# Six gate rows move from the attention's fill into the in-projection, and the fill becomes a fixed plan

## The chip, the cores and the metric

The kernel runs on one core of a Trainium2 chip. The metric is the device time of one execution in microseconds. A profile of one execution, taken by the hardware profiler, stands beside the times; its engines are TensorE (PE, with weight loads as PEld), VectorE (DVE), ScalarE (ACT), GpSimd (POOL) and SyncE (SP, which here issues nearly all DMAs).

## The reference

One layer of a hybrid encoder is computed for 1024 prompt frames and 32 sample frames (1056 columns, `T`), 1024 features wide, all in f32:

```
h = rmsnorm(x) * g_mix;  q,k,v,cb,cc,cx,ga,gc = split(h @ w_in)
y_attn = stick_breaking(q,k,v) @ w_attn_out            # 8 heads x 64
y_conv = (cb * causal_conv3(cc * cx)) @ w_conv_out
x = x + (sigmoid(ga) * y_attn + sigmoid(gc) * y_conv) @ w_o
x = x + square(relu(rmsnorm(x) @ w_up)) @ w_down
x = x + sigmoid(rmsnorm(x) @ w_ple_gate) * (p @ w_ple)
y = rmsnorm(x)
stick_breaking: A[t,s] = sigmoid(z[t,s]) * prod_{s<j<t} (1 - sigmoid(z[t,j])), strictly causal
```

The branch gates `ga` and `gc` are 1024 wide each: 16 rows of 128 features, numbered 0 to 15 here. Rows 0 to 7 belong to the attention branch and rows 8 to 15 to the convolution branch.

## The kernel before

Every f32 product is made of three matmuls on operands split into a high and a low part (fp32r), so one product of a 128x128 weight block with 264 columns is three `MATMUL 128x264`. Columns are taken in quarters of 264 (`TQ`).

**In-projection.** `SETS` lists pairs of 128-feature rows of `w_in`. The first two pairs (gate rows 0 to 3) are made plainly by `first_gates`. The other twelve (conv, query, key and value rows) go through `seven`, a Strassen-like scheme: seven block products of 24 matmuls each instead of eight, 168 matmuls for two rows. The scheme's weight sums are made by `prepare` on GpSimd, ScalarE and VectorE while the set before runs. `follow` queues the work on finished rows as generators in the list `side`, which `run` advances by a step after each product.

**The attention.** 64 turns, one for each pair of head and 128-query block (`steps`); turn n does, in the order `ORDER = "LSAFBFG"`: the reverse product scan of turn n-1 on VectorE (`weigh`, L782), the scores of turn n on TensorE (`scores`, L764 and L765, into one PSUM buffer `z`) with their sigmoid on ScalarE (L768) and mask on GpSimd (L775), the transposes of turn n-2 in two halves (`flip`, L818, copied by ScalarE at L821 and split by VectorE at L822), and every second turn the product with the values (`gather`, L839, evicted by ScalarE at L848 and VectorE at L1190). At the two places `F` the function `fill` puts in other TensorE work, so much as `shares()` allots to the turn. The query tiles of a turn (`queries`) are fetched by three DMAs on SP four turns ahead; the first two tiles are fetched just ahead of turn 0.

**The fill.** It is counted in units; one unit is 24 matmuls of 264 columns, a quarter of a gate row in plain form (`gate_group`, 96 matmuls a row). There are 60 units (`PIECES`): gate rows 4 to 15 (48), the eight rows of the per-layer embedding `p @ w_ple` (8), and two rows of the convolution's output projection (4, `conv_unit`, L937 to L939). `feed` and `weave` walk these units one after another: a unit's weights are loaded a unit or two ahead and split when the unit before begins. A group's PSUM buffer is one of two (`gps`), freed by a ScalarE copy (`sg` L652, `em` L726), and raw weights lie in four buffers (`wraw`, `RB = 4`). `START = 6` units run between the in-projection and the first turn. A finished gate row is stored raw to `gd`, fetched later as `sc` or `sa`, multiplied by the rows' inverse norm `rs` and put through the sigmoid (`branch_scale`, `branch_sigmoid`, or in `conv_unit` at L927 and L929).

The order on TensorE, VectorE, ScalarE and GpSimd is that of the program text. SP issues its DMAs in one queue, in order, and each issue can wait for a semaphore; eight semaphores are used in turn, so a DMA also waits until the eighth before it has landed.

Of the kernel before, what the change touches and what calls it, by code (L numbers as in the profile page):

```python
# [9 lines left out]
F32 = mybir.dt.float32  # L10
# [5 lines left out]
P = 128  # L16
# [21 lines left out]
SHB = 4  # L38
AT1 = (5, 4, 6, 7, 8, 12)
AT_IN = (4, 8, 10, 12, 14, 18)  # L40
PLAIN_GATES = 4
PIECES = 60.0
# [7 lines left out]
def tile_step(  # L50
# [506 lines left out]
    def conv_gate(nb, m):  # L557
# [10 lines left out]
        nc.sync.dma_start(cvd[nb, 1], m)  # L568
        yield

    def follow(nm, n, ms, wait=0):
        gens = []
        for p, m in zip((n, n + 1), ms):
            if nm in "qk":
                gens.append(keys_or_queries(nm, p, m))
            elif nm == "v":
                gens.append(values(p, m))
            elif nm == "cc":
                cst["cc", p] = m
                gens.append(call(scaled, m))  # L580
            else:
                gens.append({"cx": conv_in, "cb": conv_gate}[nm](p, m))
        side.extend([after(wait, gens[0]), after(wait + {"v": 6, "cx": 6, "cb": 4}.get(nm, 1), gens[1])])

    def first_gates():

# [72 lines left out]
    def gate_parts(n, raw):  # L659
        return even_odd(load_w(None, 0, KD, f"g{n}", raw=raw))  # L660

    def gate_unit(n, ahead):
        def body(w):
            sg = blk(f"sg{n}")
            for t in range(4):
                yield from gate_group(n, w, sg, t)
            nc.sync.dma_start(gd[n], sg)

        return partial(gate_fetch_, n), partial(gate_parts, n), body, (0, ahead), 4

    def last_gates(n):

        raw = []

        def prepare(r):
            raw.append(r[1])
            return gate_parts(n, r[0])

        def body(w):
            ww, sg = [w, None], [blk(f"sg{n}"), blk(f"sg{n + 1}")]  # L680
            ww[1] = gate_parts(n + 1, raw[0])
            for c in range(2):
                for i in range(2):
                    for t in (2 * c, 2 * c + 1):
                        yield from gate_group(n + i, ww[i], sg[i], t)
                        if c:
                            p_split(2 * i + t - 2)
                            conv_part(2 * i + t - 2)
                    if c:
                        nc.sync.dma_start(gd[n + i], sg[i])  # L690
                if c == 0:
                    p_fetch()

        return lambda: (gate_fetch_(n), gate_fetch_(n + 1)), prepare, body, (24, 2), 28

    praw, ph, pl = [], [], []

# [13 lines left out]
    def embed_unit(n):  # L711


        def prepare(raw):
            return load_w(None, 0, 2, f"pw{n}", raw=raw)

        def body(w):
            wh, wl = w
            e = blk(f"em{n}")
            for c in quarters:  # L720
                ps = group(f"ps_pw{n}{c.start}", TQ)
                for k in range(2):
                    nc.tensor.matmul(ps, wh[:, k, :], ph[k][:, c], start=k == 0, stop=False)
                    nc.tensor.matmul(ps, wh[:, k, :], pl[k][:, c], start=False, stop=False)
                    nc.tensor.matmul(ps, wl[:, k, :], ph[k][:, c], start=False, stop=k == 1)
                nc.scalar.copy(e[:, c], ps)  # L726
                if c is quarters[3]:
                    nc.sync.dma_start(ed[n], e)
                yield 0.25

        return lambda: raw_w(w_ple, n, 2, f"pw{n}"), prepare, body, (0, 2 if n < KD - 2 else 0), 1

    def keys_values(p, j):
        kk = st["k", p, j] = blk(f"ks{p}{j}", F32R, [P, SEQ])
# [148 lines left out]
    def branch_low(b):  # L883
# [2 lines left out]
        dve(lo, fetched[b][0], made[b].bitcast(F32), op=sub)  # L886
        made[b] = made[b], lo

    def branch_scale(b):
        sg = fetched[b][1]  # L890
        (pool if b[0] == "c" else dve)(sg, sg, rs, op=ALU.mult)

    def branch_sigmoid(b):
        nc.scalar.activation(fetched[b][1], fetched[b][1], AF.Sigmoid)

    def branch_group(b, t):
# [19 lines left out]
    def merge_low(n, c):  # L916
        dve(ml[n][:, c], mg[n][:, c], mh[n][:, c].bitcast(F32), op=sub)

    def conv_unit(n):

        b = "c", n

        def prepare(_):
            raw, sg = fetched[b]
            w = blk(f"cw{n}", F32R, [P, 2, 4, P])
            nc.scalar.copy(w[:, 0], raw)
            dve(sg, sg, rs, op=ALU.mult)  # L927
            dve(w[:, 1], raw, w[:, 0].bitcast(F32), op=sub)
            nc.scalar.activation(sg, sg, AF.Sigmoid)  # L929
            mg.append(sg)  # L930
            return w

        def body(w):
            for c in ts:
                ps = group(f"ps_oc{n}_{c.start}")
                for k in range(4):
                    nc.tensor.matmul(ps, w[:, 0, k, :], ch[k][:, c], start=k == 0, stop=False)  # L937
                    nc.tensor.matmul(ps, w[:, 0, k, :], cl[k][:, c], start=False, stop=False)
                    nc.tensor.matmul(ps, w[:, 1, k, :], ch[k][:, c], start=False, stop=k == 3)  # L939
                    if k == 3:  # L940
                        dve(mg[n][:, c], ps, mg[n][:, c], op=ALU.mult)
                    yield 0.165

        return int, prepare, body, (0, 1), 8

    def weave(main, other, after):

        n = 0
        for size in main:
            yield size  # L950
            n += 1 if size else 0
            if n == after - 8:
                for i in range(CFILL):
                    branch_fetch(("c", i))
            elif n >= after:
                x = next(other, None)
                if x is not None:
                    yield x
        yield from other

    SEQ_B = [("c", CFILL)]
    for n in range(KD):
        SEQ_B += [("a", n), ("c", n + CFILL + 1)] if n < KD - CFILL - 1 else [("a", n)]

    def branches_ahead(n):
        if n == LAST - 5:
            for b in SEQ_B[:2]:
                branch_fetch(b)
        elif n == LAST - 2:
            branch_scale(SEQ_B[0])  # L970
        elif n == LAST - 1:
# [58 lines left out]
        for p in range(4):  # L1030
            nc.scalar.copy(sampled[1][p // 2][:, p % 2, PAST:], ksT[p])

    units = [gate_unit(n, 1 if n == 13 else 2) for n in range(PLAIN_GATES, 14)] + [last_gates(14)]
    units += [embed_unit(n) for n in range(KD)]
    work = weave(feed(units), feed([conv_unit(n) for n in range(CFILL)]), 16 * (16 - PLAIN_GATES) + 8)
    done = 0
# [13 lines left out]
    with tc.manual_schedule(engines=MM):  # L1050
        nc.scalar.preload_act_table_set("sqrt_and_others")
        run(first_gates())
        for s_ in range(2, len(SETS)):
            nm, n = SETS[s_]
            if s_ == 2:
                side.append(after(1, stats_x()))
            elif s_ == 4:
                nc.scalar.preload_act_table_set("sigmoid_and_others")
            if s_ + 1 < len(SETS):
                side.append(prepare(f"i{s_ + 1}", AT_IN))  # L1060
            else:
                side.extend([after(4, second_parts(0)), after(6, second_parts(1)), after(7, call(next, work))])
# [80 lines left out]
    def shares():  # L1143
        base = [spare(n) for n in range(LAST + 2)]
        lo, hi = -2.0, 2.0
        for _ in range(50):
            mid = (lo + hi) / 2
            if sum(max(0.0, b + mid) for b in base) < PIECES - START:
# [22 lines left out]
    with tc.manual_schedule(engines=MM):  # L1171
        queries(0, 0, 0)
        queries(0, 0, 1)
        for n in range(LAST + 3):
# [31 lines left out]
                split_high(p, c)  # L1206
            branches_ahead(n)
            if n == LAST + 1:
                for _ in work:
                    pass  # L1210
                split_high(3, slice(0, 768))
        for f in pending + split_low:
            f()
# [798 lines left out]
```

## Time and profile before

| | |
|---|---|
| times | 1574.42 us median of 3 (1573.56 to 1577.35) |
| profiled execution | 1574.38 us, its span 1572.7 us |
| PE, DVE, ACT, POOL busy | 98%, 67%, 47%, 21% of the span |
| TensorE's granted clock | 0.993 over the span |
| in-projection | 0 to about 312 us |
| six fill units, then turns 0 to 63 | to 329.9 us, then to about 616 us |
| output projections, MLP, embedding | about 616 us to the end |

The numbers are read like this: busy time is the union of an engine's instructions; TensorE's matmuls overlap in its pipeline, so its busy share says how rarely it stood still and not how fast it went. Idle time of an engine matters only where TensorE in turn waits for it.

### The profile page before, as it was taken

To read this page: it belongs to the slowest core of one execution; us is meant where nothing else is said; L and a number is where in the kernel's file an instruction comes from. 1 tells how busy PE (TensorE), PEld (TensorE's weight loads), DVE (VectorE), ACT (ScalarE), POOL (GpSimd) and SP (SyncE) were. 2 spreads that over 40 slices of the span, in tenths; PEclk is the share of its full clock that TensorE was granted. 3 is DMA by queue.
4 is the path that set the end of the run, shared out by engine and by line. 5 is a ranking of instruction groups with operands and counts; after the bars stand their busy time and mean duration, and the time that the engine had idled before them with its cause. 6 is when DMAs were issued, how large, how long until landed. Compare 5 with 4: busy or idle time off the path is not lost.

```text
span 1572.7 us, 29473 instructions
## 1 busy us (share of the span) xinstructions
PE 1535.2 (98%) x11880; PEld 1520.4 (97%) x11880; DVE 1050.9 (67%) x1401; ACT 737.3 (47%) x1341; POOL 332.3 (21%) x346
## 2 busy tenths in 40 slices
PE   8999999999999989999999999999999999999996
PEld 7999999999999978999999999999999999999996
DVE  7568566656666665774668555555577986799866
ACT  6644443444444554333355555555643334344544
POOL 2223332011111112101412222222020221013353
PEclk9999999999999999999999999999999999999998
DMA  6513455373433733354444434444886897673442
GB/s 225 200 55 129 163 196 189 92 235 115 123 109 102 274 124 117 123 183 156 163 163 163 144 137 144 150 151 148 289 284 203 273 332 249 200 265 97 136 135 104
DMA packets 110521, 268.96 MB, mean 171 GB/s; under 512 B 13072, under 2 KB 30096, under 8 KB 110384
## 3 DMA queue, kind: packets, MB, share of 16 engines
q1 hardware_dynamic: 110240, 267.05, 50.0%
q8 instruction: 93, 1.52, 0.4%
q14 instruction: 44, 0.36, 0.1%
q10 hardware_dynamic: 144, 0.03, 0.0%
HBM read 186.31 MB, written 80.72 MB: 170 GB/s over the span
## 4 chain that ended last, share of the span: by engine, by line
PE 88%; DVE 5%; DMA 2%; ACT 2%; issue 1%; POOL 1%; SPq 0%; DVEq 0%; ACTq 0%; POOLq 0%
PE ps_dn L1627 6%; PE ps_dn L1625 6%; PE ps_dn L1626 6%; PE ps_A11u L213 4%; PE ps_A11u L214 4%; PE ps_A11u L215 4%; PE ps_g L648 3%; PE ps_g L649 3%; PE ps_g L650 3%; PE ps_A11i L215 3%; PE ps_A11i L213 3%; PE ps_A11i L214 3%; PE av L839 2%; PE ps_wo L1316 2%; PE ps_wo L1315 2%; PE ps_wo L1314 2%
## 5 line engine op out<-in xcount | busy, mean ns | idle before, releaser
L1627 PE MATMUL ps_dn<-fh,wlo_dn 128*128 128x264 f32 x896 | 255.3, 285 | 2.4 <-DVE wlo_dn L1518 2.4
L1625 PE MATMUL ps_dn<-fh,whi_dn 128*128 128x264 f32 x896 | 254.8, 284 | 0.0
L1626 PE MATMUL ps_dn<-fl,whi_dn 128*128 128x264 f32 x896 | 254.8, 284 | 0.0
L1627 PEld LDWEIGHTS ps_dn<-fh,wlo_dn 128*128 128x128 f32 x896 | 168.6, 188 | 3.0 <-DVE wlo_dn L1518 2.8
L1625 PEld LDWEIGHTS ps_dn<-fh,whi_dn 128*128 128x128 f32 x896 | 168.6, 188 | 0.1
L1626 PEld LDWEIGHTS ps_dn<-fl,whi_dn 128*128 128x128 f32 x896 | 168.6, 188 | 0.0
L648 PE MATMUL ps_g<-B,whi_g 128*128 128x264 f32 x384 | 115.4, 301 | 0.0
L649 PE MATMUL ps_g<-B,whi_g 128*128 128x264 f32 x384 | 109.4, 285 | 0.0
L650 PE MATMUL ps_g<-B,wlo_g 128*128 128x264 f32 x384 | 109.1, 284 | 0.0
L822 DVE TENSOR_TENSOR at<-pa,at 128x512 fp32r<-128x512 f32 (+2 forms) x96 | 53.0, 554 | 57.9 <-ACT at L821 57.5
L1518 DVE TENSOR_TENSOR wlo_dn<-raw_dn,whi_dn 128x1024 fp32r<-128x1024 f32 x40 | 69.8, 1744 | 29.7 <-ACT whi_dn L1512 29.7
L775 POOL TENSOR_SCALAR_AFFINE_SELECT r<-r 128x128 f32<-128x128 f32 x64 | 28.3, 442 | 283.0 <-ACT r L768 275.7
L782 DVE TENSOR_TENSOR_SCAN r<-r 128x128 f32<-128x128 f32 (+3 forms) x64 | 87.7, 1371 | 0.1
L200 POOL TENSOR_TENSOR s_u<-raw_u,raw_u 128x512 f32<-128x512 f32 x30 | 44.6, 1487 | 185.1 <-DVE slS_u L163 184.8
L1512 ACT CAST whi_dn<-raw_dn 128x1024 fp32r<-128x1024 f32 x40 | 42.0, 1050 | 78.8 <-PE ps_dn L1626 78.4
L1570 POOL TENSOR_TENSOR c<-c,rs 128x528 f32<-128x528 f32 x16 | 26.7, 1668 | 245.0 <-DVE c L1634 123.0
L648 PEld LDWEIGHTS ps_g<-B,whi_g 128*128 128x128 f32 x384 | 72.4, 188 | 0.7 <-ACT sg L652 0.5
L649 PEld LDWEIGHTS ps_g<-B,whi_g 128*128 128x128 f32 x384 | 72.4, 189 | 0.0
L200 POOL TENSOR_TENSOR s_i<-raw_i,raw_i 128x512 f32<-128x512 f32 x24 | 33.0, 1376 | 186.2 <-DVE slS_i L163 156.1
L650 PEld LDWEIGHTS ps_g<-B,wlo_g 128*128 128x128 f32 x384 | 72.3, 188 | 0.0
L1538 DVE TENSOR_TENSOR fl<-mr,fh 128x1056 fp32r<-128x1056 f32 x56 | 69.9, 1248 | 0.0
L213 PE MATMUL ps_A11u<-T,shS_u 128*128 128x264 f32 x240 | 68.5, 285 | 0.0
(430 smaller groups left out, 5451.7 us busy)
## 6 DMA issues: line engine op xcount, KB each, us to landing
raw_dn<-in_w_down_dram SPq DMA_DIRECT2D x56, 512.0 KB, 4.6
mr<-mdT SPq DMA_DIRECT2D x32, 528.0 KB, 5.8
raw_u<-in_w_up_dram SPq DMA_DIRECT2D x32, 512.0 KB, 3.6
raw_i<-in_w_in_dram SPq DMA_DIRECT2D x28, 512.0 KB, 4.4
mdB<-m SPq DMA_DIRECT2D x48, 264.0 KB, 2.5
mr<-mdB SPq DMA_DIRECT2D x24, 528.0 KB, 6.2
raw_pg<-in_w_ple_gate_dram SPq DMA_DIRECT2D x17, 512.0 KB, 3.5
gd<-sg SPq DMA_DIRECT2D x16, 528.0 KB, 4.1
```

What stands on the lines that cost most here:

```text
L200: f()
L213: nc.tensor.matmul(p_, wh[:, k, :], o[:, 0, c], start=new and n == 0, stop=False, **on)
L214: nc.tensor.matmul(p_, wh[:, k, :], o[:, 1, c], start=False, stop=False, **on)
L215: nc.tensor.matmul(p_, wl[:, k, :], o[:, 0, c], start=False, stop=z, **on)
L648: nc.tensor.matmul(ps, wh[:, k, :], o[:, 0, q], start=i == 0, stop=False)
L649: nc.tensor.matmul(ps, wh[:, k, :], o[:, 1, q], start=False, stop=False)
L650: nc.tensor.matmul(ps, wl[:, k, :], o[:, 0, q], start=False, stop=i == 7)
L782: nc.vector.tensor_tensor_scan(rev, rev, rev, 1.0, ALU.mult, ALU.bypass)
L1538: dve(l, mraw.pop(v), opd[v].bitcast(F32), op=sub)
L1625: nc.tensor.matmul(ps, hi[:, j, :], oh, start=j == 0, stop=False)
L1626: nc.tensor.matmul(ps, hi[:, j, :], ol, start=False, stop=False)
L1627: nc.tensor.matmul(ps, lo[:, j, :], oh, start=False, stop=j == NP_ - 1)
```

## The change

- **Three more pairs in `SETS`.** Gate rows 4 and 5 come after the first half of the q, k, v and conv rows, 6 and 7 after the second q, k, v, and 8 and 9 at the end. They go through `seven`, 168 matmuls a pair, and no longer stand in the fill, where a pair took 192.
- **They are finished there.** `gate_done` multiplies such a row by `rs` on VectorE (1056 columns), two steps later applies the sigmoid on ScalarE, and stores the finished gate to `gd`. `READY = (4, ..., 9)` tells the later stages to skip scaling and sigmoid for them: the attention branch's rows 4 to 7 and the convolution's first two rows, which are the two in the fill.
- **The fill is a list.** `plan` holds pieces (six matmuls of a gate or embedding row, three of a conv row) and `hooks` holds what is to happen at piece i: loads 28 to 40 pieces ahead of use, splits mostly 12 to 5 pieces ahead. Its sum is about 36 units instead of 60. The embedding's weights come in two loads of 512 KB, not eight of 128 KB. From the seventh embedding piece on, embedding and conv pieces alternate in proportion.
- **`START` is 3**, not 6, and `shares()` spreads the rest, 33 units instead of 54, over the turns.
- **`branches_ahead`** fetches the first branch's tiles 8 turns before the end instead of 5, scales 4 instead of 2 and applies the sigmoid 2 instead of 1 before it.

```diff
-START = 6
+START = 3
+READY = (4, 5, 6, 7, 8, 9)
-    SETS = [("g", 0), ("g", 2)] + [(nm, 0) for nm in ("cc", "cx", "cb", "q", "k", "v")]
-    SETS += [(nm, 2) for nm in ("q", "k", "v", "cc", "cx", "cb")]
+    SETS = [("g", 0), ("g", 2)] + [(nm, 0) for nm in ("cc", "cx", "cb", "q", "k", "v")] + [("g", 4)]
+    SETS += [(nm, 2) for nm in ("q", "k", "v")] + [("g", 6)] + [(nm, 2) for nm in ("cc", "cx", "cb")] + [("g", 8)]
...
+    def gate_done(n, m):
+        scaled(m)
+        yield
+        yield
+        nc.scalar.activation(m, m, AF.Sigmoid)
+        nc.sync.dma_start(gd[n], m)
+        yield
...
+    def plan_gates(ns):
+        for n in ns[:-2]:
+            i = len(plan)
+            hook(i - 32, partial(gate_fetch, n))
+            hook(i - 12, partial(gate_split, n))
+            for t in range(4):
+                put(gate_pieces(n, t), 0.25, 4)
+            hook(len(plan), partial(gate_store, n))
...
+    def embed_fetch(g):
+        raw = ew[g] = wraw.tile([P, 8, P], F32, tag="raw", name=f"raw_pw{g}")
+        nc.sync.dma_start(raw.rearrange("p (n k) c -> p n k c", k=2), w_ple[4 * g : 4 * g + 4].rearrange("n p k c -> p n k c"))
...
     def branch_sigmoid(b):
+        if gate_ready(b):
+            return
         nc.scalar.activation(fetched[b][1], fetched[b][1], AF.Sigmoid)
...
+        hook(i0 - 40, partial(embed_fetch, 0), partial(embed_fetch, 1))
+        hook(i0 - 6, partial(embed_split, 0))
+        hook(i0 + 2, partial(embed_split, 1))
...
+                    hook(i - 28, partial(branch_fetch, ("c", n)))
+                    hook(i - 9, partial(conv_high, n))
+                    hook(i - 7, partial(conv_low, n))
+                    hook(i - 5, partial(conv_gates, n))
...
     def fill(upto):
         nonlocal done
-        while done < upto - 0.12:
-            done += next(work, 1.0)
+        while done < upto - 0.12 and turn_n[0] < len(plan):
+            hooks_to(turn_n[0])
+            size, f = plan[turn_n[0]]
+            turn_n[0] += 1
+            f()
+            done += size
```

Three places in the order of instructions matter for what follows. Names: `q000` is the query tile for turns 0 and 1, `q001` that for turns 2 and 3; `raw_pw` is an embedding weight as loaded; `m1_i16` and `m2_i16` are gate rows 8 and 9; `sg10` is a fill gate row; `kk` holds the sample's keys; `r000` is turn 0's sigmoid output.

SP's queue at the attention's start, before:

```order
L1026 DMA kk1_3899<-in_ckT_dram 128x256 x2
L750 DMA q000_4111<-qd_164 64x2x256
L751 DMA q000_4111<-qd_164 64x256
L752 DMA q000_4111<-qd_164 64x256
L750 DMA q001_4115<-qd_164 64x2x256
L751 DMA q001_4115<-qd_164 64x256
L752 DMA q001_4115<-qd_164 64x256
L750 DMA q002_4119<-qd_164 64x2x256
```

and the same place with the change:

```order
L773 DMA q000_4736<-qd_164 64x2x256
L774 DMA q000_4736<-qd_164 64x256
L775 DMA q000_4736<-qd_164 64x256
L773 DMA q001_4740<-qd_164 64x2x256
L774 DMA q001_4740<-qd_164 64x256
L575 DMA gd_143<-m1_i16_4366 128x1056
L575 DMA gd_143<-m2_i16_4367 128x1056
L775 DMA q001_4740<-qd_164 64x256
L773 DMA q002_4744<-qd_164 64x2x256
```

The stores of gate rows 8 and 9 now stand between the second and the third load of `q001`.

ScalarE at the same place, before, from the last fill copy ahead of turn 0 on:

```order
L652 COPY sg5_4020<-ps_g5_1_4055 128x264
L1031 COPY kk0_3898<-ks0_173 128x32
L1031 COPY kk0_3898<-ks1_174 128x32
L1031 COPY kk1_3899<-ks2_175 128x32
L1031 COPY kk1_3899<-ks3_176 128x32
L768 ACTIVATE r000_4126<-z000_4123 128x128
```

and with the change, from the copy of the third of the three `START` units on:

```order
L659 COPY sg10_4625<-ps_g10_2_4683 128x264
L574 ACTIVATE m1_i16_4366<-m1_i16_4366 128x1056
L1072 COPY kk0_4619<-ks0_173 128x32
L1072 COPY kk0_4619<-ks1_174 128x32
L1072 COPY kk1_4620<-ks2_175 128x32
L1072 COPY kk1_4620<-ks3_176 128x32
L574 ACTIVATE m2_i16_4367<-m2_i16_4367 128x1056
L791 ACTIVATE r000_4751<-z000_4748 128x128
```

Two sigmoids of 1056 columns now stand between that copy and turn 0's own sigmoid.

SP's queue at the embedding's weights, before, where they follow the store of the last gate row of the fill:

```order
L874 DMA sc0_6977<-gd_143 128x1056
L874 DMA sc1_6981<-gd_143 128x1056
L862 DMA cv30_6985<-cvd_167 128x1056
L862 DMA cv31_6987<-cvd_167 128x1056
L690 DMA gd_143<-sg15_6388 128x1056
L99 DMA raw_pw2_6990<-in_w_ple_dram 128x256
L99 DMA raw_pw3_7059<-in_w_ple_dram 128x256
```

and with the change, where the loads stand among the query tiles of the second head (`q012` is for its turns 4 and 5):

```order
L98 DMA raw_g15_5236<-in_w_in_dram 128x1024
L773 DMA q012_5039<-qd_164 64x2x256
L774 DMA q012_5039<-qd_164 64x256
L775 DMA q012_5039<-qd_164 64x256
L736 DMA raw_pw0_5797<-in_w_ple_dram 128x4x256
L759 DMA ks10_5154<-kd_165 64x1024 x2
L773 DMA q013_5150<-qd_164 64x2x256
```

The first embedding load moved from behind the last gate row's store to some 30 turns ahead of its use.

More of the change, by code (lines that the diff above doesn't have):

```diff
@@ L660, in gate_parts @@
         return even_odd(load_w(None, 0, KD, f"g{n}", raw=raw))
-    def gate_unit(n, ahead):
-        def body(w):
-            sg = blk(f"sg{n}")
-            for t in range(4):
[L666 to L688, printed above, removed]
-                    if c:
[L690 to L694, printed above, removed]
+    plan, hooks = [], {}
@@ new lines, in tile_step, with hook, put, gate_fetch @@
+    graw, gw, gsg = {}, {}, {}
+    def hook(i, *fs):
+        hooks.setdefault(i, []).extend(fs)
+    def put(gen, size, count):
+        plan.extend([(size, partial(next, gen, None))] * count)
+    def gate_fetch(n):
+        graw[n] = gate_fetch_(n)
+    def gate_split(n):
+        gw[n] = gate_parts(n, graw.pop(n))
+    def gate_pieces(n, t):
+        if n not in gsg:
+            gsg[n] = blk(f"sg{n}")
+        yield from gate_group(n, gw[n], gsg[n], t)
+    def gate_store(n):
+        nc.sync.dma_start(gd[n], gsg.pop(n))
@@ L709, in p_split, with embed_split, embed_pieces @@
         dve(pl[f][:, c], praw[f][:, c], ph[f][:, c].bitcast(F32), op=sub)
[L711 to L731, printed above, removed]
+    ew = {}
+    def embed_fetch(g):
+        raw = ew[g] = wraw.tile([P, 8, P], F32, tag="raw", name=f"raw_pw{g}")
+        nc.sync.dma_start(raw.rearrange("p (n k) c -> p n k c", k=2), w_ple[4 * g : 4 * g + 4].rearrange("n p k c -> p n k c"))
+    def embed_split(g):
+        ew[g] = load_w(None, 0, 8, f"pw{g}", raw=ew[g])
+    def embed_pieces(n):
+        wh, wl = ew[n // 4]
+        e, j = blk(f"em{n}"), 2 * (n % 4)
+        for c in quarters:
+            ps = group(f"ps_pw{n}{c.start}", TQ)
+            for k in range(2):
+                nc.tensor.matmul(ps, wh[:, j + k, :], ph[k][:, c], start=k == 0, stop=False)
+                nc.tensor.matmul(ps, wh[:, j + k, :], pl[k][:, c], start=False, stop=False)
+                nc.tensor.matmul(ps, wl[:, j + k, :], ph[k][:, c], start=False, stop=k == 1)
+            nc.scalar.copy(e[:, c], ps)
+            if c is quarters[3]:
+                nc.sync.dma_start(ed[n], e)
+            yield
     def keys_values(p, j):
@@ L917, in merge_low @@
         dve(ml[n][:, c], mg[n][:, c], mh[n][:, c].bitcast(F32), op=sub)
[L919 to L959, printed above, removed]
+    cw = {}
+    def conv_high(n):
+        w = cw[n] = blk(f"cw{n}", F32R, [P, 2, 4, P])
+        nc.scalar.copy(w[:, 0], fetched["c", n][0])
+        if not gate_ready(("c", n)):
+            dve(fetched["c", n][1], fetched["c", n][1], rs, op=ALU.mult)
@@ new lines, in conv_low, with conv_gates, conv_pieces @@
+    def conv_low(n):
+        w = cw[n]
+        dve(w[:, 1], fetched["c", n][0], w[:, 0].bitcast(F32), op=sub)
+    def conv_gates(n):
+        branch_sigmoid(("c", n))
+        mg.append(fetched["c", n][1])
+    def conv_pieces(n):
+        w = cw.pop(n)
+        for c in ts:
+            ps = group(f"ps_oc{n}_{c.start}")
+            for k in range(4):
+                nc.tensor.matmul(ps, w[:, 0, k, :], ch[k][:, c], start=k == 0, stop=False)
+                nc.tensor.matmul(ps, w[:, 0, k, :], cl[k][:, c], start=False, stop=False)
+                nc.tensor.matmul(ps, w[:, 1, k, :], ch[k][:, c], start=False, stop=k == 3)
+                if k == 3:
+                    dve(mg[n][:, c], ps, mg[n][:, c], op=ALU.mult)
+                yield
@@ new lines, in plan_rest @@
+    def plan_rest():
+        es = [(n, embed_pieces(n)) for n in range(KD)]
+        cs = [(n, conv_pieces(n)) for n in range(CFILL)]
+        e_, c_ = 4 * KD, 12 * CFILL
+        i0, ne, nc_ = len(plan), 0, 0
+        hook(i0 - 40, partial(embed_fetch, 0), partial(embed_fetch, 1))
+        hook(i0 - 6, partial(embed_split, 0))
+        hook(i0 + 2, partial(embed_split, 1))
+        while ne < e_ or nc_ < c_:
+            if ne < e_ and (ne < 6 or nc_ == c_ or (ne - 6) * c_ <= nc_ * (e_ - 6)):
+                put(es[ne // 4][1], 0.25, 1)
+                ne += 1
+            else:
+                n = nc_ // 12
+                if nc_ % 12 == 0:
+                    i = len(plan)
+                    hook(i - 28, partial(branch_fetch, ("c", n)))
+                    hook(i - 9, partial(conv_high, n))
+                    hook(i - 7, partial(conv_low, n))
+                    hook(i - 5, partial(conv_gates, n))
+                put(cs[n][1], 0.165, 1)
+                nc_ += 1
@@ L1031, in sample_keys, with hooks_to @@
             nc.scalar.copy(sampled[1][p // 2][:, p % 2, PAST:], ksT[p])
[L1033 to L1036, printed above, removed]
+    plan_gates([n for n in range(4, 16) if n not in READY])
+    plan_rest()
+    total = sum(size for size, _ in plan)
+    place, done = min(hooks), 0.0
+    def hooks_to(i):
+        nonlocal place
+        while place <= i:
+            for f in hooks.pop(place, ()):
+                f()
+            place += 1
+    turn_n = [0]
     def fill(upto):
         nonlocal done
-        while done < upto - 0.12:
-            done += next(work, 1.0)
+        while done < upto - 0.12 and turn_n[0] < len(plan):
+            hooks_to(turn_n[0])
+            size, f = plan[turn_n[0]]
+            turn_n[0] += 1
+            f()
+            done += size
     def ahead(n):
@@ L1147, in shares @@
             mid = (lo + hi) / 2
-            if sum(max(0.0, b + mid) for b in base) < PIECES - START:
+            if sum(max(0.0, b + mid) for b in base) < total - START:
                 lo = mid
@@ L1208, in tile_step @@
             if n == LAST + 1:
-                for _ in work:
-                    pass
+                fill(2 * total)
+                hooks_to(len(plan))
                 split_high(3, slice(0, 768))
```

32 lines of the change are left out of this document (24 added, 8 removed).

## Prediction

> **What bounds the kernel now.** I read the page's head first, then busy time by stretches.
>
> ```profile
> span 1572.7 us, 29473 instructions
> PE   8999999999999989999999999999999999999996
> PEclk9999999999999999999999999999999999999998
> core 0: us, PE busy (x) PEld busy (x) DVE busy (x) ACT busy (x) POOL busy (x), PEclk, DMA share, GB/s
> 200.00:240.00 40.00, 40.00 (x331) 39.99 (x331) 25.45 (x35) 19.56 (x44) 12.09 (x8) 1.00 0.52 192
> 480.00:520.00 40.00, 40.00 (x318) 39.13 (x318) 24.97 (x31) 19.55 (x40) 6.46 (x20) 1.00 0.40 122
> 520.00:560.00 40.00, 34.80 (x255) 32.74 (x254) 25.74 (x38) 22.26 (x54) 4.51 (x17) 0.96 0.75 259
> 560.00:600.00 40.00, 36.07 (x246) 33.59 (x246) 28.94 (x44) 22.41 (x56) 8.14 (x19) 0.96 0.33 119
> 600.00:640.00 40.00, 37.44 (x237) 36.39 (x238) 21.33 (x33) 15.67 (x28) 5.54 (x3) 0.96 0.38 135
> ```
>
> TensorE is the bound nearly everywhere: in the in-projection (200 to 240 us) and in most of the attention (480 to 520 us) it stands still for nothing while VectorE is busy 25 us of 40. The exception is the attention's last third: from 520 to 640 us it is idle for 5.2 + 3.9 + 2.6 = 11.7 us, and the granted clock's mean is 0.96. I cut that piece finer.
>
> ```profile
> 540.00:555.00 15.00, 9.89 (x70) 8.98 (x70) 9.50 (x14) 8.57 (x21) 1.03 (x4) 1.00 0.79 298
> 555.00:558.40 3.40, 3.40 (x14) 2.91 (x13) 2.10 (x3) 1.08 (x4) 0.00 (x0) 0.50 0.14 39
> 576.00:582.20 6.20, 3.61 (x26) 3.23 (x25) 4.70 (x8) 3.95 (x10) 0.29 (x1) 1.00 0.14 48
> 582.30:585.70 3.40, 3.40 (x16) 3.38 (x14) 0.99 (x2) 1.71 (x4) 0.58 (x3) 0.50 0.95 334
> 612.00:616.30 4.30, 2.41 (x19) 2.20 (x18) 3.33 (x6) 3.72 (x8) 0.00 (x0) 1.00 0.76 247
> 616.40:619.80 3.40, 3.40 (x14) 3.40 (x13) 0.78 (x2) 0.00 (x0) 2.43 (x1) 0.50 1.04 409
> 1440.00:1444.00 4.00, 2.35 (x20) 2.14 (x19) 4.00 (x4) 0.93 (x2) 3.18 (x1) 1.00 0.31 79
> 1444.00:1447.40 3.40, 3.40 (x30) 3.40 (x29) 2.40 (x5) 1.24 (x2) 0.92 (x1) 1.00 0.29 119
> ```
>
> Three idle pieces (5.1, 2.6 and 1.9 us) are each followed by 3.4 us at half clock, which costs half of that, 1.7 us. An idle piece of 1.65 us at 1440 us has no such tail (the last two rows). Which waits make these pieces is told by the chain of work and by TensorE's waits between 320 and 640 us (total, times, longest).
>
> ```profile
> 540.47 8.33 DMA raw_pw<-in_w_ple_dram
> 552.58 1.17 DVE sc L927
> 553.74 0.61 DVE cw L928
> 577.92 1.18 DVE sc L927
> 579.12 1.08 ACT sc L929
> 613.93 0.98 ACT sa L894
> 614.94 0.38 ACT avl L848
> ```
>
> ```profile
> PE ps_pw L723 <- ACT em L726: 6.3, 6, 2.6
> PE ps_oc L117 <- DVE oT L1213: 1.9, 1, 1.9
> PE ps_oc L937 <- ACT em L726: 1.1, 2, 0.6
> PE z L764 <- issue: 0.5, 1, 0.5
> ```
>
> The 5.1 us piece is an embedding weight that takes 8.33 us from issue to landing, and then conv weights prepared just before use. The 2.6 us piece is a gate's scaling and sigmoid (1.18 + 1.08 us) in ScalarE's queue ahead of a copy that frees an embedding group's PSUM buffer. The 1.9 us piece is the end: the last head's output waits behind a sigmoid of 0.98 us.
>
> **The change, part by part.**
>
> *Fewer products.* Six rows cost 6 x 96 = 576 matmuls in the fill; three pairs through `seven` cost 3 x 168 = 504. A matmul of 264 columns takes 40.00 / 331 = 0.121 us in the in-projection. ScalarE's copies of two fill units in a row show the same:
>
> ```profile
> 320.65 0.38 ACT L652 COPY sg<-ps_g 128x264 f32<-128x264 f32 x1 [2.53 <-PE ps_g L650]
> 323.56 0.38 ACT L652 COPY sg<-ps_g 128x264 f32<-128x264 f32 x1 [2.53 <-PE ps_g L650]
> 329.72 0.57 ACT L1031 COPY kk<-ks 128x32 f32<-128x32 f32 x4
> ```
>
> The first two lie 2.91 us apart, 24 x 0.121. So 72 matmuls less are **-8.7 us**, the in-projection growing by 61 us and the attention with its start shrinking by 70.
>
> *Weight sums, scaling and sigmoid in the in-projection.* Per pair these are the sums and splits of any set, two scalings of about 1.2 us and two sigmoids of about 1.1 us, in 20.3 us of TensorE work. A set's VectorE now takes 25.45 of 40 us, ScalarE 19.56, so TensorE hides them: **0**. Were that cover gone, three pairs would cost at most 3 x 2 x 2.3 = 14 us. Their twins in the attention's end go: two scalings and two sigmoids there lie on the chain above.
>
> *The late loads and splits.* Embedding weights are loaded about 30 turns ahead; the conv weights' three steps are spread over pieces; the two conv gates need no scaling nor sigmoid. I take the first two pieces away with their clock tails: 5.1 + 2.6 + 2 x 1.7 = **-11.1 us**. ScalarE's order at the end puts the last head's copy (`avl`) ahead of the 0.98 us sigmoid: **-0.9 us**. What is late next is that same end (1.9 - 0.9 us, its tail kept in the sum) and the short waits on `em` copies, 6.3 + 1.1 less the two removed, about 2 us, which are in both.
>
> *The attention's start.* This is where I see a new wait. In the order above, two stores of gate rows 8 and 9 stand in SP's queue between the second and the third load of `q001`, which turn 2's second matmul reads. The second store waits for the second sigmoid, which on ScalarE stands behind the copy at the end of the `START` units, the first sigmoid and the `kk` copies: 0.38 + 1.08 + 0.57 + 1.08 = 3.1 us after that end. Then the load is issued (about 0.4 us behind) and lands:
>
> ```profile
> q<-qd SPq DMA_DIRECT2D x6, 64.0 KB, 3.2
> gd<-sg SPq DMA_DIRECT2D x1, 528.0 KB, 5.2
> ```
>
> These are the medians between 305 and 330 us. The load goes behind two 528 KB stores, so between 3.2 and 5.2 us: turn 2 can begin 6.7 to 8.7 us after the `START` units. By TensorE's own work (two turns of scores with 6 matmuls each, 0.73 us) it would begin after 1.9 us. That is 4.8 to 6.8 us of waiting; I take 5.3, near the small load's own row, since the first store is issued two microseconds earlier. Such a wait is above every idle piece that was followed by a half clock, so 1.7 us more; 0.5 us of issue wait existed before. **+6.5 us**, with ends at 0 (the query lands early, if the sigmoids run while TensorE is still in the `START` units) and 9 us (6.8 + 1.7 + 0.5).
>
> [...]
>
> *Thinner cover in the attention.* The fill falls from 54/66 = 0.82 to 33/66 = 0.50 units a turn, 0.93 us less. Turns now:
>
> ```profile
> L764 PE MATMUL z<-ks,q x96: 219/341/628, 329.9 to 597.3; 128*128 128x384 f32 x24, 128*128 128x512 f32 x24, 128*128 128x320 f32 x16, 128*128 128x448 f32 x16
> L109 DVE TENSOR_TENSOR wlo_g<-raw_g,whi_g 128x1024 fp32r<-128x1024 f32 x6 | 7.4, 1226 | 3.7 <-ACT whi_g L108 3.7
> ```
>
> 63 turns in 267 us, less the 11.1 us above, is 4.07 us a turn; it becomes 3.14. VectorE's 24.97 of 40 us is 2.54 us a turn, less 0.1 for the fewer splits `wlo_g` (1.23 us, one in four units): 2.44 of 3.14, 78% where it was 62%. At 62% TensorE waited for nothing; in the stretch 560 to 600 us, with VectorE at 72%, it idled 3.9 us, 1.3 of them outside the 2.6 us piece. That rate over 64 x 3.14 = 201 us would be 6.7 us. Those waits belong to the short embedding groups, which fill a third of the new plan (12 of 36 units). So a third of the rate, **+2 us**, with ends 0 and 7. A gain is excluded: nothing waits in the turns now.
>
> Sum: -8.7 - 11.1 - 0.9 + 6.5 + 2 = -12.2. From the profiled execution's own 1574.4 us, which is also the median, that gives **1562 us**.
>
> **The rivals.**
>
> 1. *No wait at the start.* For it: TensorE waits only 0.5 us there now. Against: the stores stand ahead of the load in a queue that runs in order. 1562 - 6.5 = **1556 us**.
> [...]
> 3. *Both prices at their upper ends*, 7 and 9 us: 1562 + 5 + 2.5 = **1570 us**. For it: VectorE at 78% with a chain of four engines a turn.
> 4. *The late waits stay*: the change does not do what it says, because two 512 KB embedding loads wait for one of four weight buffers, or the conv steps still bunch. 1562 + 11 = **1573 us**, within measurement of no change.
> 5. *Slower: the turn stops being TensorE's.* If scan, copies and splits hold each turn at some length above 3.14 us, the cover taken out becomes idle time. For it: ScalarE, VectorE and TensorE release each other in every turn. Against: each scan's result is read two turns later. It decides at (4.7 + 12.2 + 2) / 64 = 0.3 us a turn; at 3.6 us a turn it adds 64 x 0.46 = 29 us in place of 2: **1589 us**.
>
> **How the numbers follow.** Chances: forecast 0.48, rival 1 0.18, rival 2 0.08, rival 3 0.13, rival 4 0.06, rival 5 0.07. A measurement here tells about 0.3%, 4.7 us, from no change: faster means below 1569.7. Forecast, rivals 1 and 2 and half of rival 3 are faster: 0.80. The other half and rival 4 are the same: 0.13. Rival 5 is slower: 0.07. The range takes in rival 1 with its cover cost at 0 (1554, less 1 for the end's clock) and rival 3 with 1 us more: 1553 to 1571; it leaves out rivals 4 and 5.
>
> **What the changed profile would show.** The first turn's scores begin at about 330 + 61 - 9 = 382 us. SP has two `gd` stores ahead of a query load there, TensorE waits about 5 us in turns 0 to 2, and a half clock of 3.4 us follows. No wait of TensorE leads to `raw_pw`, and none to a gate's scaling. From turn 5 on TensorE is busy in nine tenths of the time or more and VectorE in three quarters; the first product of the output projections comes at about 604 us instead of 616. The prediction is wrong if TensorE waits for `r` (scan) or `z` in every turn, if the pairs' sets in the in-projection take more than 20.3 us each, or if `q001` is there in time.

## The result and the profile after

The changed kernel takes 1559.38 us (median of four, 1558.56 to 1561.65), the kernel before 1575.04 us beside it: a ratio of 0.9902, 95% interval 0.9884 to 0.9919. The prediction was 1562, range 1553 to 1571, faster at 0.80. A second measurement of the unaltered changed kernel gave 0.9917 (0.9903 to 0.9931). The two profiled spans, 1572.7 and 1556.8 us, lie 15.9 us apart. One of the five executions of the kernel with eight rows, below, took 1725.85 us at a granted clock of 0.803 where all others had 0.990 to 0.997; its time and ratio are those of the other four.

The page's head, and busy time by stretches (the columns are those of the prediction's rows):

```profile
span 1556.8 us, 29396 instructions
PEclk9999999999999999999999999999999999999998
...
200.00:240.00 40.00, 40.00 (x331) 39.99 (x331) 24.74 (x34) 19.38 (x42) 12.10 (x8) 1.00 0.42 155
320.00:360.00 40.00, 40.00 (x329) 39.80 (x328) 26.98 (x40) 14.54 (x36) 6.05 (x4) 1.00 0.24 67
380.00:420.00 40.00, 34.84 (x271) 32.81 (x270) 24.68 (x39) 21.09 (x50) 8.59 (x24) 0.96 0.64 192
480.00:520.00 40.00, 40.00 (x321) 39.05 (x320) 32.92 (x43) 24.35 (x53) 7.73 (x25) 1.00 0.69 213
520.00:560.00 40.00, 39.99 (x298) 38.23 (x298) 33.84 (x47) 27.41 (x64) 9.20 (x27) 1.00 0.72 221
560.00:600.00 40.00, 36.50 (x275) 34.81 (x275) 34.83 (x52) 27.00 (x62) 12.30 (x20) 1.00 0.31 107
```

TensorE stood still for 11.7 us in the attention's last third before. Now it works through from 520 to 560 us (39.99 of 40 us), although VectorE is busy 85% of that stretch, and idles 3.5 us from 560 to 600. The longer in-projection (320 to 360 us) has no idle time either. A new hole of 5.2 us stands at the attention's opening (380 to 420 us, clock 0.96). TensorE's waits between 380 and 640 us (total, times, longest):

```profile
PE z L788 <- DMA q<-qd: 3.1, 1, 3.1
PE z L787 <- DMA q<-qd: 2.0, 1, 2.0
PE ps_oc L116 <- DVE oT L1268: 1.9, 1, 1.9
PE ps_oc L971 <- ACT em L751: 0.8, 1, 0.8
PE ps_pw L748 <- DVE sc L975: 0.7, 1, 0.7
```

Five waits, 8.5 us, and no more. No `raw_pw`, no gate scaling and no weight split of the conv rows is among them (`sc` at L975 is VectorE taking a conv product out of PSUM, times its finished gate; it is not a gate's scaling). SP's queue at the opening shows what the third load of `q001` stood behind, and when it went out:

```profile
381.07 0.60 SPq L774 DMA_DIRECT2D q<-qd  x1
383.02 1.78 SPq L575 DMA_DIRECT2D gd<-m_i  x2
384.86 0.48 SPq L775 DMA_DIRECT2D q<-qd  x1
```

The attention's first scores come at 383.6 us and the first product of the output projections at 599.65 us, 286.0 us apart before and 216.0 us now.

### The profile page after: what moved, and what is told of

It is laid out like the page before. It is cut to its first block, busy times and chain, and to the rows that moved or that the text cites. A ratio compares the mean times of both kernels' runs of the same rounds, so it can differ in the third digit from the quotient of the medians.

```text
span 1556.8 us, 29396 instructions
## 1 busy us (share of the span) xinstructions
PE 1522.7 (98%) x11808; PEld 1509.5 (97%) x11808; DVE 1066.9 (69%) x1425; ACT 739.9 (48%) x1347; POOL 363.1 (23%) x358
## 5 line engine op out<-in xcount | busy, mean ns | idle before, releaser
L199 POOL TENSOR_TENSOR s_i<-raw_i,raw_i 128x512 f32<-128x512 f32 x30 | 40.8, 1359 | 223.5 <-DVE slS_i L162 193.0
L798 POOL TENSOR_SCALAR_AFFINE_SELECT r<-r 128x128 f32<-128x128 f32 x64 | 39.8, 622 | 196.4 <-ACT r L791 196.4
L213 PE MATMUL ps_A11u<-T,shS_u 128*128 128x264 f32 x240 | 68.5, 286 | 0.0
L212 PE MATMUL ps_A11u<-T,shS_u 128*128 128x264 f32 x240 | 68.5, 285 | 0.0
L214 PE MATMUL ps_A11i<-T,slS_i 128*128 128x264 f32 x240 | 68.4, 285 | 0.0
L212 PE MATMUL ps_A11i<-T,shS_i 128*128 128x264 f32 x240 | 68.3, 285 | 0.0
L213 PE MATMUL ps_A11i<-T,shS_i 128*128 128x264 f32 x240 | 68.2, 284 | 0.0
L214 PE MATMUL ps_A11u<-T,slS_u 128*128 128x264 f32 x240 | 68.2, 284 | 0.0
L162 DVE TENSOR_TENSOR slS_i<-s_i,shS_i 128x512 fp32r<-128x512 f32 x45 | 36.0, 804 | 45.7 <-ACT shS_i L160 45.3
```

The costliest lines, as they stand in the source:

```text
L212: nc.tensor.matmul(p_, wh[:, k, :], o[:, 0, c], start=new and n == 0, stop=False, **on)
L213: nc.tensor.matmul(p_, wh[:, k, :], o[:, 1, c], start=False, stop=False, **on)
L214: nc.tensor.matmul(p_, wl[:, k, :], o[:, 0, c], start=False, stop=z, **on)
```

## The experiments

Each is timed against the kernel before on the same chip; "span" is that of the profiled execution. Ratios compare across groups of runs, single medians only within one.

**The plan alone.** All gate rows are back in the fill, six units ahead of the attention; the plan and the earlier fetch of the first branch's tiles stay.

```diff
-READY = (4, 5, 6, 7, 8, 9)
+READY = ()
...
-START = 3
+START = 6
...
-    SETS = [("g", 0), ("g", 2)] + [(nm, 0) for nm in ("cc", "cx", "cb", "q", "k", "v")] + [("g", 4)]
-    SETS += [(nm, 2) for nm in ("q", "k", "v")] + [("g", 6)] + [(nm, 2) for nm in ("cc", "cx", "cb")] + [("g", 8)]
+    SETS = [("g", 0), ("g", 2)] + [(nm, 0) for nm in ("cc", "cx", "cb", "q", "k", "v")]
+    SETS += [(nm, 2) for nm in ("q", "k", "v")] + [(nm, 2) for nm in ("cc", "cx", "cb")]
```

> The fixed plan with its loads alone: all twelve rows 4 to 15 are made in the fill again, six units ahead of the attention as in the kernel before. Theory A: the late loads, splits and gate waits of the kernel before are 9.6 us of idle time and two half clocks (3.4 us), of which the changed kernel's trace shows 1.5 us left: 1575.0 - 11.5 = 1563.5 us, TensorE idle under 2 us between turn 5 and turn 62. Rival: the plan's loads help only together with the shorter fill (the conv gates then still need scaling and sigmoid here, in VectorE's queue): 1566 to 1572 us.

Measured: 1566.29 us, ratio 0.9959 (0.9946 to 0.9971), span 1563.2. TensorE's waits in that kernel between 300 and 640 us:

```profile
PE ps_g L657 <- DVE wlo_g L108: 2.2, 1, 2.2
PE ps_oc L116 <- DVE oT L1268: 1.9, 1, 1.9
PE ps_pw L748 <- ACT em L751: 1.9, 4, 0.9
PE z L787 <- issue: 0.5, 1, 0.5
PE ps_oc L971 <- ACT em L751: 0.4, 1, 0.4
```

The kernel before had, beside its `em` waits, two on the conv weights:

```profile
PE ps_oc L939 <- DVE cw L928: 1.4, 1, 1.4
...
PE ps_oc L937 <- ACT cw L926: 1.0, 1, 1.0
```

The late waits are gone with the plan alone, as theory A says (`em` 7.4 us before, 2.3 now; the two `cw` waits of 2.4 us gone), but a new one of 2.2 us came: it ends with the first gate row's split (`wlo_g`), which VectorE runs behind three other operations (1.31, 0.22 and 0.76 us). The span falls by 9.5 us; idle time falls by 5.1 us and three half clocks are gone (granted clock 0.996 over the span, 0.993 before; 1.7 us each, 5.1 us, by an estimate). One of the three, at the end, is gone although the 1.9 us wait is still there (last section). The median falls less, 0.41%, 6.5 us, which as a time is the rival's expectation and not theory A's 11.5 us. The profiled execution, 1564.88 us, is one of the two shortest of five; the longest, 1568.23 us, had a granted clock of 0.994 where it had 0.996. That is the size of two half clocks (an estimate: 1.7 us each, 0.001 of the span), but those executions were not traced.

**The two stores moved.** Rows 8 and 9 are stored behind turn 3's loads.

```diff
+    stores = []
...
-        nc.sync.dma_start(gd[n], m)
+        if n < 8:
+            nc.sync.dma_start(gd[n], m)
+        else:
+            stores.append((n, m))
...
+            if n == 3:
+                for n_, m_ in stores:
+                    nc.sync.dma_start(gd[n_], m_)
```

> The changed kernel (1559.4 us) with only the two stores of gate rows 8 and 9 moved, from SP's queue between the second and third load of q001 to behind turn 3's loads. Theory A, from the trace after: the opening wait has two causes, the first query load landing late (2.0 us at turn 0) and the stores (3.1 us at turn 2, then 1.7 us by the half clock). Then 2.0 us at turn 0 stays, the 3.1 us go, and the half clock goes or stays: 1554.6 to 1556.3 us. Theory B, the prediction's: the stores make all of the wait: 5.2 + 1.7 us go, 1552.5 us. Theory C: the third load lands late because the transfers are slow, not because of the stores ahead of it: 1559.4 us.

Measured: 1554.10 us, ratio 0.9883 (0.9870 to 0.9897), span 1552.2. The waits at the opening are now these:

```profile
PE z L792 <- ACT r L796: 1.4, 1, 1.4
...
PE z L792 <- ACT sg L664: 0.5, 1, 0.5
```

The 3.1 us behind the stores and the half clock are gone (granted clock 0.995 over the span, 0.994 in the trace after), so theory C falls. Theory B falls too: 1.9 us stay. They are not the landing that theory A named, though. Turn 1's scores need the one `z` buffer that turn 0's sigmoid (`r`) frees, and that sigmoid stands in ScalarE's queue behind the two gate sigmoids of 1.09 us and the `kk` copies. In the trace after, this wait was covered by the late landing. The interval of the ratio overlaps that of the changed kernel's first measurement, so it is the trace, 4.6 us shorter in span, that decides between the theories.

**Six units ahead of the attention** (`START = 6`, nothing else).

> The changed kernel with six fill units ahead of the attention instead of three (30 units left for the turns instead of 33). Theory A: 8.7 us more of TensorE work cover both causes of the opening wait, 2.0 + 3.1 us, and its half clock, 1.7 us: 1559.4 - 6.8 = 1552.6 us. By the prediction's price of the thinner cover (2 us for 21 units fewer) 3 units fewer cost 0.3 us: 1552.9. Rival: the turns are at the edge of their cover and give the three units back as waits, 3 x 2.9 less what VectorE leaves: up to 1559.

Measured: 1555.62 us, ratio 0.9888 (0.9873 to 0.9903), span 1553.4. The loads are hidden and the half clock at the opening is gone (granted clock 0.995 over the span, 0.994 in the trace after). The second gate sigmoid now falls just ahead of turn 0's (1.2 us of wait at turn 1), and new waits of 0.2 to 0.6 us appear in the turns, the longest of them the last row here:

```profile
PE z L787 <- ACT r L791: 1.2, 1, 1.2
...
PE av L862 <- DVE at L845: 0.6, 1, 0.6
```

TensorE idles three microseconds less, not five, and the time lies between theory A's 1552.6 us and the rival's 1559.

**The end's PSUM buffer.** The rotation of the output projections' buffers starts with one that the attention doesn't hold.

```diff
-    pools[:] = [gps2, gps, gps2]
+    turn[0] = 0
+    pools[:] = [gps, gps2, gps2]
```

> The changed kernel with only the rotation of the output projections' PSUM buffers turned by one, so that the first of their groups uses a buffer that the attention does not hold. Theory A: the 1.9 us at the attention's end and the half clock behind it (1.7 us) come from that buffer, held until the last head's output is written: both go, 1559.4 - 3.6 = 1555.8 us. Rival: the next group meets the same wait 3 us later, or another wait takes its place (weights, gate): 1557.5 to 1559.4 us.

Measured: 1556.85 us, ratio 0.9894 (0.9881 to 0.9908), span 1555.1. The 1.9 us wait on `oT` and the half clock behind it are gone (the granted clock, 0.994 over the span as in the trace after, has its half clocks at the opening, below), and no wait takes their place: theory A. The ratio alone would not show it, since its interval overlaps the changed kernel's. Only 1.7 of the 3.6 us reach the span, since in this execution the unaltered opening cost more. Busy time in three stretches of 3.41 us there:

```profile
384.68:388.09 3.41, 1.42 (x9) 1.16 (x9) 1.12 (x2) 0.76 (x3) 0.58 (x2) 1.00 0.91 316
388.10:391.51 3.41, 1.41 (x6) 1.33 (x7) 0.00 (x1) 0.65 (x2) 0.12 (x1) 0.50 0.44 117
391.52:394.92 3.40, 3.40 (x15) 3.10 (x15) 1.96 (x4) 0.86 (x2) 0.74 (x4) 0.50 0.93 233
```

The same wait for `q001` (3.6 us here) lies across two stretches and brings two of them at half clock where the trace after had one: 1.7 us more, and 0.3 us more idle time.

**Opening and end mended together.** Rows 8 and 9 get sigmoid and store in turns 3 and 4, and the rotation is turned.

```diff
+    late = []
+
+    def gate_out(n, m):
+        nc.scalar.activation(m, m, AF.Sigmoid)
+        nc.sync.dma_start(gd[n], m)
...
-        nc.scalar.activation(m, m, AF.Sigmoid)
-        nc.sync.dma_start(gd[n], m)
+        if n < SETS[-1][1]:
+            gate_out(n, m)
+        else:
+            late.append(partial(gate_out, n, m))
...
+            if n in (3, 4):
+                late.pop(0)()
...
-    pools[:] = [gps2, gps, gps2]
+    turn[0] = 0
+    pools[:] = [gps, gps2, gps2]
```

> The changed kernel with the opening and the end mended together: rows 8 and 9 get their sigmoid and store at turns 3 and 4 of the attention, and the output projections' PSUM rotation is turned by one. Theory A (three causes at the opening: the stores ahead of q001, the two sigmoids in ScalarE's queue ahead of turn 0's sigmoid, which frees the scores' PSUM for turn 1, and 0.5 us for the last fill copy; at the end the PSUM buffer): against the run with the stores moved, 1552.2 us of span, 1.4 us go at turn 1 and 1.9 + 1.7 us at the end: a span of 1547.2, a time of 1549 to 1550 us. Rival: the two sigmoids, 2.2 us of ScalarE, hold turns 3 and 4 instead, or the first query's landing shows once they are gone: a span of 1549 us.

Measured: 1549.91 us, ratio 0.9851 (0.9838 to 0.9864), span 1548.3. All of TensorE's waits from 380 to 640 us:

```profile
PE ps_oc L979 <- ACT em L759: 0.8, 1, 0.8
PE ps_pw L756 <- DVE sc L983: 0.7, 1, 0.7
PE z L795 <- ACT sg L667: 0.5, 1, 0.5
```

Theory A by the waits; the span is 1.1 us longer than it expected. There is no half clock in the attention any more (granted clock 0.996 over the span, 1.00 from 420 to 580 us), and the kernel beats both others; its interval lies below the changed kernel's.

**Thinner cover.** On that kernel, one or two more pairs go to the in-projection, next to other gate pairs there (the lines of `SETS` are not shown), and in two runs three more fill units go ahead of the turns.

```diff
-READY = (4, 5, 6, 7, 8, 9)
+READY = (4, 5, 6, 7, 8, 9, 10, 11)            # eight rows
+READY = tuple(range(4, 14))                    # ten rows
```

> The kernel with the opening and the end mended, and rows 10 and 11 made by seven products in the in-projection too: the fill falls from 33 to 25 units in the turns. By the count of matmuls, 24 x 0.121, it is 2.9 us faster than that kernel; by what 21 units were worth between the plan alone and the changed kernel (about 3.0 us each in the turns) 3.6 us. Rival, the price of thinner cover: a turn becomes 2.8 us, of which VectorE needs some 2.4, and the short embedding groups wait: 0 to 2 us slower than without the pair.

> The same with rows 12 and 13 too: 17 units in the turns, ten rows made ready. By matmuls it is 5.8 to 7.2 us faster than the kernel with the opening and the end mended. Rival: a turn is now 2.4 us of TensorE's work, as long as VectorE's own 2.4 us, so VectorE becomes the bound: TensorE waits for scans and splits in most turns, and the pair gives nothing or costs up to 15 us.

> The kernel with the opening and the end mended, with six fill units ahead of the attention instead of three (30 left for the turns). Theory A: its opening waits for 0.5 us only and its turns for 1.5 us, so there is nothing to hide: no change, 1549.9 us within 2. Rival: three units ahead were too few for the loads of turns 0 to 4, 2 us faster; or the turns miss the units, 2 us slower.

> Eight rows made ready, with six units ahead of the attention (22 in the turns). In the run with three units the opening waited 1.8 us and a half clock of 3.4 us followed (1.7 us). Theory A: three more units hide both and the turns at 22 units wait no more than 1 us beyond the 1.4 us they showed at 25: 1549.2 - 3.5 + 1 = 1546.7 us. Rival: the waits of the ten-row run (8 us in the turns at 17 units) begin here: 1550 us.

| rows ready, units ahead | units left for the turns | time, us | ratio (interval) | span, us | idle, 380 to 640 us |
|---|---|---|---|---|---|
| 6, 3 | 33 | 1549.91 | 0.9851 (0.9838 to 0.9864) | 1548.3 | 2.1 |
| 6, 6 | 30 | 1550.03 | 0.9857 (0.9840 to 0.9873) | 1548.2 | 3.0 |
| 8, 3 | 25 | 1548.43 | 0.9842 (0.9828 to 0.9856) | 1548.2 | 3.2 |
| 8, 6 | 22 | 1554.52 | 0.9885 (0.9870 to 0.9899) | 1552.4 | 6.1 |
| 10, 3 | 17 | 1557.30 | 0.9897 (0.9882 to 0.9912) | 1556.2 | 10.0 |

Busy time of the turns from 420 to 580 us (last row: from 436; the granted clock's mean from 420 to 460 us is 0.91 there), one row of each kernel: the changed one (33 units), then 30, 25, 22 and 17:

```profile
420.00:580.00 160.00, 159.92 (x1263) 155.05 (x1262) 129.22 (x174) 97.62 (x220) 41.05 (x100) 1.00 0.55 171
420.00:580.00 160.00, 159.06 (x1251) 154.15 (x1252) 133.07 (x181) 99.61 (x225) 40.10 (x106) 1.00 0.54 167
420.00:580.00 160.00, 158.77 (x1248) 152.91 (x1247) 141.92 (x200) 105.17 (x237) 42.85 (x112) 1.00 0.59 178
420.00:580.00 160.00, 156.03 (x1205) 148.31 (x1206) 141.54 (x200) 104.52 (x238) 36.40 (x114) 1.00 0.59 177
436.00:580.00 144.00, 139.72 (x1068) 131.44 (x1067) 133.55 (x191) 97.47 (x222) 40.78 (x110) 1.00 0.63 190
```

With VectorE at 81% (33 units) TensorE waits for 0.1 us of 160; at 89% it waits for 1.2 us (25 units), at 88% for 4.0 (22 units), at 93% for 4.3 of 144. So VectorE's share alone does not tell when the waits begin; in these runs they grow between 25 and 22 units. There the waits have the form the prediction's fifth rival describes, here in the ten-row run between 430 and 600 us:

```profile
PE av L870 <- DVE at L853: 2.5, 5, 0.9
PE pa L849 <- DVE r L813: 1.9, 4, 0.6
PE z L795 <- ACT r L799: 1.5, 4, 0.5
```

With six rows, three more units ahead change nothing, as expected. The fourth pair is worth nothing that can be measured (the intervals overlap): 2.9 us fewer products, against 1.2 us more idle time and, in the traced execution, a half clock (1.7 us; granted clock 0.995 against 0.996) at the opening. The fifth costs: ten rows take 7.4 us more than six, as their rival said, where the products alone would give 5.8 us less. Adding three units ahead to eight rows, expected at 1546.7, made it slower, against theory A: 2.9 us more idle time than with three. From six to eight rows at six units ahead, the idle time (+3.1), a half clock (+1.7; granted clock 0.995 against 0.996) and the products (-2.9) give +1.9 us of the +4.2 in the spans; the rest stays open.

**The changed kernel again.**

> The changed kernel unaltered, beside the others. All theories: 0.990 of the kernel before. On the half clock: if it is set on a fixed grid of 3.41 us by TensorE's idle share of the window before, then every window with 1.9 us or more of idle time is followed by one at half clock, and none with 1.8 us or less; the opening wait then brings one or two of them, the 1.9 us at the end one or none, by where the grid falls.

Measured: 1559.64 us, ratio 0.9917, span 1560.6, 3.8 us longer than the first profile of the same kernel, with less idle time (8.3 us against 8.7 between 380 and 640 us). Half clocks make the difference: 17.1 us in five stretches instead of 6.8 in two (granted clock 0.991 over the span against 0.994), worth 5.1 us more by an estimate; less the 0.4 us of idle time that is 4.7 us, and 0.9 us of it stays open. Two of the five, from 386.15 and from 590.95 us, follow a stretch with only 1.6 and 1.5 us of idle time, so the expected bound of 1.8 us is too sharp. The opening waits are these, of 4.8 us in all:

```profile
PE z L788 <- DMA q<-qd: 2.9, 1, 2.9
...
PE z L787 <- ACT r L791: 1.4, 1, 1.4
...
PE z L787 <- ACT sg L659: 0.5, 1, 0.5
```

So here too, as with the stores moved, it is turn 0's sigmoid and not the first query's landing that makes the second part of the wait.

## Why the prediction was right, point by point

Each term, with what the two spans and their idle times show for it:

| step | predicted, us | measured, us | worked out from |
|---|---|---|---|
| fewer products | -8.7 | -10.6 | plan alone against changed: attention 63.0 us shorter without idle time, in-projection with start 52.4 longer |
| late loads and splits | -11.1 | -11.7 | idle 9.8 to 1.5 us, two half clocks of 1.7 |
| the end | -0.9 | 0 | wait 1.89 before, 1.92 after |
| opening | +6.5 | +6.4 | idle 0.5 to 5.2 us, one half clock of 1.7 |
| thinner cover | +2 | 0 | 0.1 us idle of 160 |
| sum | -12.2 | -15.9 | spans 1572.7 and 1556.8 |

**In-projection, 0:** right. TensorE is busy in all of 320 to 360 us, and three sets with three units fewer take 52.4 us by the trace against 3 x 20.3 - 8.7 = 52.2 forecast.

**Fewer products:** the count is right and the unit's worth is a little low. 21 units fewer shorten the attention by 63.0 us, 3.0 a unit where 24 x 0.121 gives 2.9. What adds the 0.09 us per unit in the turns was not found.

**Late loads:** the mechanism and the size are right. The two pieces and their clock tails went, and most of the short `em` waits with them, which the prediction kept. The run of the plan alone shows that the plan does this without the moved rows: these waits fall there by 7.5 us of idle time and two half clocks, 11.0 us. Its span gains 9.5 us, since its opening has a wait of its own.

**Opening:** the place, the two stores, the half clock and the size are right (5.2 us of idle time against 5.3). The cause is right for three fifths of it, 3.1 us. The other two are the first query's landing in the trace after, and, where that is earlier, as in the second trace of the same kernel, turn 0's sigmoid behind two gate sigmoids. The step that failed here is the one that took ScalarE's queue as a delay for the store alone: the same 3.1 us delay `r`, which frees the only `z` buffer.

**Thinner cover:** the mis-sized term, +2 that was 0. The rate was taken from 560 to 600 us, where VectorE was at 72% and TensorE idled. That idle time came from single late operations and not from VectorE's load: at 81% in the regular turns there is 0.1 us in 160, and at 85% from 520 to 560 us none. The upper end of 7 us is near what 17 units cost (10.0 us of idle time less 3.5 at the opening), not 33.

**The end:** the term -0.9 failed. The step "ScalarE's order puts `avl` ahead of the 0.98 us sigmoid" holds and gains nothing. ScalarE, and then VectorE, at the end of the attention:

```profile
596.65 0.84 ACT L1223 CAST o3h<-oT 128x768 fp32r<-128x768 f32 x1
597.39 0.22 ACT L869 COPY oT<-osT 128x32 f32<-128x32 f32 x1
597.51 0.62 ACT L903 CAST whi_oa<-raw_oa 128x512 fp32r<-128x512 f32 x1
598.15 0.37 ACT L871 COPY avl<-av 64x256 f32<-64x256 f32 x1
598.42 1.08 ACT L924 ACTIVATE sa<-sa 128x1056 f32<-128x1056 f32 x1
...
598.40 0.68 DVE L909 TENSOR_TENSOR wlo_oa<-raw_oa,whi_oa 128x512 fp32r<-128x512 f32 x1
599.12 0.48 DVE L1268 SCALAR_TENSOR_TENSOR oT<-av,vlast,avl 64x256 f32<-64x256 f32 x1
```

Three other copies stand ahead of `avl`, and the split `wlo_oa` stands between `avl` and the `oT` that frees the buffer. The first product came at 599.65 us, not 604, by the terms above.

**The rivals.** No wait at the start (1556) fell, and the run with opening and end mended shows that the wait could be had down to 0.5 us. That the clock stays whole at the opening (1560 us, chance 0.08) neither trace of the changed kernel shows: behind waits of 2.0 and 3.1 us the first has 3.40 us at a granted clock of 0.50, from 389.32 us on, and the second has 3.41 us at 0.50 from 386.15 us on. Both prices at their upper ends fell: the opening cost 6.4 us and the cover nothing. Late waits staying fell. The slower one, a turn bound by other engines, is real but begins below 25 units, where the changed kernel keeps 33; its point of decision, set at 0.3 us a turn, was far from reached. The sum came out 3.7 us too high, and by little luck: four of the five terms erred the same way, and only the end, 0.9 us, the other.

## What to carry to other kernels

A delay in an engine's queue has to be followed to every consumer behind it: the two sigmoids, 1.09 us each, delayed a store and a load, and also a PSUM buffer. Price thin cover from a stretch where the same loop runs without late single operations; here TensorE waited for 0.1 to 0.9 us of 160 with VectorE at 81 to 83%, and for 1 to 4 us at 88 to 89%. Work moved out of a covered stretch pays until the cover is used up: here three pairs paid, the fourth (25 units left) gave nothing measurable, and the fifth (17) cost more than it saved.

## What the hardware showed

Between 100 and 1528 us the traces before and after show five stretches at half clock, each 3.41 us long. In the trace after they start at 389.32 and 600.94 us, 62 x 3.413 apart; in the trace before at 554.96, 582.27 and 616.40, 8 and 10 x 3.413 apart. The 3.41 us just ahead of them hold 3.1 and 1.9 us of TensorE's idle time after, 2.3, 2.0 and 1.9 us before. The same 1.9 us wait at the end, in the changed kernel (first two rows) and with the plan alone (last two):

```profile
597.53:600.94 3.41, 1.49 (x10) 1.29 (x9) 2.49 (x4) 2.38 (x5) 0.00 (x0) 1.00 0.97 312
600.95:604.35 3.40, 3.40 (x14) 3.40 (x13) 0.53 (x1) 0.00 (x0) 1.61 (x1) 0.50 0.89 303
...
602.70:606.11 3.41, 2.21 (x19) 2.00 (x17) 2.96 (x5) 3.04 (x7) 0.00 (x0) 1.00 0.56 172
606.12:609.53 3.41, 2.69 (x16) 2.69 (x17) 1.51 (x4) 1.01 (x2) 0.66 (x1) 1.00 0.99 384
```

In the changed kernel 1.9 us stand idle in the first row, and the second is at half clock; with the plan alone 1.2 and 0.7 us stand idle in the two rows, and both are at full clock. How much idle time a half clock follows these runs do not settle: it followed 1.6 and 1.5 us in the second trace of the changed kernel (stretches from 382.73 and 587.53 us), but not 1.65 us in the trace before (1440 to 1444 us) nor 1.67 us in the trace after (1423.55 to 1426.96 us). With the PSUM rotation turned, a stretch at half clock that had 2.0 us of idle time in it was followed by another (388.10 to 394.92 us); the five in the traces before and after had none in them, and full clock followed each. So the price of one wait can differ by 1.7 us (an estimate: half of one such stretch) from run to run of the same kernel.
